# First products of a two-layer trunk's MLPs computed token-wise, their outputs turned by VectorE and a DRAM scratch

## The chip, the core and the metric

The kernel runs on one core of one Trainium2 chip. A core has TensorE for matrix products (into PSUM), VectorE (DVE) and ScalarE (ACT) for work on elements, GpSimd (POOL), SyncE (SP), which issues DMAs here, and 16 DMA engines between the device's memory (DRAM) and the core's SBUF. Each engine serves its own queue in order and waits on semaphores. The metric is the device time of one execution in microseconds, smaller is better. The program was run three times; one further execution was recorded by the hardware profiler, and all rows below come from it.

## What is computed

256 tokens of width 2048 go through two layers. In each layer a mixer (recurrent in the first, latent attention in the second, with a memory attention beside it) is followed by an MLP with squared ReLU, each between two RMS norms with a residual. Cut to the part that the change touches:

```python
D_MODEL = 2048; SEQ = 256; DEPTH = 2; D_FF = 4 * D_MODEL

def rms_norm(x, g):
    xf = x.astype(jnp.float32)
    xf = xf * lax.rsqrt(jnp.mean(xf * xf, axis=-1, keepdims=True) + EPS)
    return xf.astype(x.dtype) * g

def reference(x, mem, positions, ...):
    h = x
    for layer in range(DEPTH):
        ...
        h = h + rms_norm(y, g_mix_post[layer])
        f = rms_norm(h, g_mlp_pre[layer]) @ w_ff1[layer]
        f = jnp.square(jax.nn.relu(f)) @ w_ff2[layer]
        h = h + rms_norm(f, g_mlp_post[layer])
    return h
```

All of it is float32: w_ff1 is 2048 x 8192 and w_ff2 8192 x 2048 in each layer.

## The kernel before

**Products in three parts.** A float32 value is held as a high part, rounded to TensorE's fast float32 type, and a low part, the rest. A product is the sum of high x high, high x low and low x high. Weights come from DRAM as raw tiles of 128 x 1024 (`wraw`, five buffers, line 167, on SP's queue), ScalarE casts each to `whi` (line 129) and VectorE subtracts to get `wlo` (line 136), four buffers each. One such tile is a *group*: for 512 output columns it holds two k-tiles of 128 rows. `feed_high` and `feed_low` convert and load as far ahead as the buffers allow: a conversion waits until TensorE has used the group four back, a load until VectorE has converted the raw tile five back.

**Two forms of a product.** `gemm` walks over the groups of one weight block. *Feature-wise* (`by_features`) the weights are the stationary operand and the tokens run past: for each k-tile and each 128 features one matmul of 512 columns, token high and low parts side by side (line 235), and one of 256 (line 236). The output has features on partitions, in one PSUM bank for each 128 features; the two halves of a bank are added afterwards (`join`, lines 289 and 291: ScalarE copies a half to `corr`, VectorE adds). *Token-wise* (`by_tokens`) 128 tokens are stationary and the weights run past: for each k-tile and each of the two token halves three matmuls of 512 columns (lines 247 to 249). The output has tokens on partitions.

**The MLP.** `mlp` cuts the 8192 hidden features into NB = 8 blocks of 1024. `up(b)` makes block b from X, the normed tokens (features on partitions), in two products of 512 features, sixteen k-tiles, eight groups each; `down(b, F)` multiplies it with its rows of w_ff2 in four products of 512 columns, four groups each, token-wise, and adds up in `y`. The second product needs hidden features on partitions, which is how the feature-wise first product leaves them. The order is up(0), up(1), down(0), up(2), down(1), ... up(7), down(6), down(7). After the last matmul of each 128 features `ev` joins the two halves into `fs`; `square` then makes max(s, 0) x s on VectorE (line 726), casts the high part on ScalarE (line 727) and subtracts for the low part (line 729), into a tile F of 512 features.

**The order of the work.** It is written out by hand. Work beside the products stands as generators in a queue `bg`: at each group `run(1)` starts one more of them and takes each that has yielded 1 a step further, ahead of that group's conversion on VectorE and its load on SP, and behind its cast on ScalarE; `run(2)` does so behind the group's matmuls for those that yielded 2. So a step's place in an engine's queue is set by the group in which it falls.

**The second MLP's start.** The last product of the mixer before it is made with its second token half behind the first (`Mixed`), so that residual, transposes of `h` on TensorE (line 604) and split into high and low parts of the first token half run beside the second half's matmuls. The last four transposes and parts of X stand right ahead of up(0).

## Time and profile before

| | |
|---|---|
| median of three runs | 2126.18 us (2125.41 to 2127.99) |
| profiled execution | 2128.45 us |
| its span, from the first to the last instruction | 2126.7 us |
| TensorE, VectorE, ScalarE busy | 2092.9, 1326.0, 1074.0 us |
| DMA | 403.36 MB, 190 GB/s on average |

Busy time of TensorE is counted from a matmul's start to its modelled end; matmuls overlap, so a busy share near one says that there are few holes, not how fast the matmuls follow each other. How far apart they start is read from the timeline, and how long a stage lasts from the start of its first matmul to the start of the next stage's first.

### The profile page before, as it was taken

Reading aid. Unit: us, or ns where it says so; the run is one execution under the profiler, and the core shown is the slowest. Engines: PE = TensorE matmul, PEld = TensorE weight load, DVE = VectorE, ACT = ScalarE, POOL = GpSimd, SP = SyncE. Lnnn points to the kernel's source line nnn. Section 1 sums busy time; section 2 is a strip of 40 time slices with the busy share of each in tenths; the row PEclk is TensorE's granted clock in tenths of the full one; section 3 lists DMA queues with packets and bytes.
Section 4 is the critical chain, followed back from the end, with each engine's and each line's share of the span. In section 5 each row is a group of like instructions: output and inputs, shape, how many; then the busy total and the mean of one; then the engine's idle time right before and its main releaser. Section 6 shows DMA issues by size and latency. Waiting matters only on the chain. (4 is left out here: it accounts for less than half of the span.)

```text
span 2126.7 us, 29075 instructions
## 1 busy us (share of the span) xinstructions
PE 2092.9 (98%) x11055; PEld 1796.3 (84%) x11055; DVE 1326.0 (62%) x1960; ACT 1074.0 (50%) x1677; POOL 81.9 (4%) x124
## 2 busy tenths in 40 slices
PE   8999999999999999999999999999999999999998
PEld 6888888888888888888889898888888888888886
DVE  5688856764656656566576766576555656556565
ACT  6577645654444444444467655464543444434443
POOL 2311100000000000000010000000000000000001
PEclk9999999999999999999999999999999999999999
DMA  9565765666666666668656544656666666666664
GB/s 347 160 177 170 246 196 182 189 187 193 190 189 190 187 190 190 189 194 266 192 153 190 150 141 149 201 170 187 191 186 196 189 189 190 187 192 190 191 189 129
DMA packets 208604, 403.36 MB, mean 190 GB/s; under 512 B 12614, under 2 KB 31184, under 8 KB 206416
## 3 DMA queue, kind: packets, MB, share of 16 engines
q1 hardware_dynamic: 204720, 381.99, 60.5%
q0 software_dynamic: 3168, 18.47, 2.4%
q8 instruction: 86, 1.41, 0.3%
q10 hardware_dynamic: 576, 1.05, 0.1%
q14 instruction: 54, 0.44, 0.1%
HBM read 395.16 MB, written 6.29 MB: 189 GB/s over the span
## 5 line engine op out<-in xcount | busy, mean ns | idle before, releaser
L136 DVE TENSOR_TENSOR wlo<-wraw,whi 128x1024 fp32r<-128x1024 f32 x662 | 811.6, 1227 | 666.0 <-ACT whi L129 665.5
L129 ACT CAST whi<-wraw 128x1024 fp32r<-128x1024 f32 x662 | 692.4, 1046 | 832.1 <-PE psa L249 364.5
L235 PE MATMUL psb<-X,whi 128*128 128x512 f32 x2808 | 1002.7, 401 | 4.7 <-DVE ga L291 3.8
L236 PE MATMUL psb<-X,wlo 128*128 128x256 f32 x2808 | 788.8, 281 | 0.0
L235 PEld LDWEIGHTS psb<-X,whi 128*128 128x128 f32 x2808 | 528.8, 188 | 135.0 <-DVE ga L291 4.7
L247 PE MATMUL psa<-whi,X 128*128 128x512 f32 (+3 forms) x1636 | 605.8, 370 | 1.5 <-ACT whi L131 1.3
L248 PE MATMUL psa<-wlo,X 128*128 128x512 f32 (+3 forms) x1636 | 602.8, 368 | 0.6 <-DVE wlo L136 0.6
L249 PE MATMUL psa<-whi,X 128*128 128x512 f32 (+3 forms) x1636 | 602.6, 368 | 0.0
L236 PEld LDWEIGHTS psb<-X,wlo 128*128 128x128 f32 x2808 | 531.6, 189 | 1.1
L247 PEld LDWEIGHTS psa<-whi,X 128*128 128x128 f32 x1636 | 309.0, 189 | 52.8 <-ACT whi L131 1.7
L248 PEld LDWEIGHTS psa<-wlo,X 128*128 128x128 f32 x1636 | 308.9, 189 | 50.2 <-DVE wlo L136 1.0
L249 PEld LDWEIGHTS psa<-whi,X 128*128 128x128 f32 x1636 | 308.9, 189 | 50.1
L289 ACT COPY corr<-psb 128x256 f32<-128x256 f32 x192 | 68.6, 373 | 33.4 <-PE psb L236 33.2
L751 DVE SCALAR_TENSOR_TENSOR y<-psa,r,y 128x512 f32<-128x512 f32 (+1 forms) x114 | 79.2, 734 | 1.6 <-PE psa L249 1.5
L138 DVE SCALAR_TENSOR_TENSOR wlo<-wraw,pB,whi 128x384 fp32r<-128x384 f32 (+2 forms) x80 | 44.0, 599 | 23.0 <-ACT whi L131 22.8
L729 DVE TENSOR_TENSOR X<-fs,X 128x256 fp32r<-128x256 f32 x128 | 53.6, 419 | 0.0
L726 DVE SCALAR_TENSOR_TENSOR fs<-fs 128x256 f32<-128x256 f32 x128 | 53.5, 418 | 0.0
L138 DVE SCALAR_TENSOR_TENSOR wlo<-wraw,pM,whi 128x512 fp32r<-128x512 f32 x64 | 45.5, 755 | 12.8 <-ACT whi L131 12.5
L131 ACT ACTIVATE whi<-wraw,pB 128x384 fp32r<-128x384 f32 (+2 forms) x80 | 43.0, 597 | 17.2 <-PE psa L249 15.5
L727 ACT CAST X<-fs 128x256 fp32r<-128x256 f32 x128 | 51.3, 401 | 0.0
L291 DVE TENSOR_TENSOR fs<-psb,corr 128x256 f32<-128x256 f32 x128 | 48.2, 418 | 1.5
L131 ACT ACTIVATE whi<-wraw,pM 128x512 fp32r<-128x512 f32 x64 | 42.4, 718 | 10.0 <-PE psa L249 5.0
(279 smaller groups left out, 752.8 us busy)
## 6 DMA issues: line engine op xcount, KB each, us to landing
wraw<-in_w_ff_dram SPq DMA_DIRECT2D x512, 512.0 KB, 3.7
wraw<-in_w_o_dram SPq DMA_DIRECT2D x64, 512.0 KB, 3.8
wraw<-in_a_w_in_dram SPq DMA_DIRECT2D x56, 512.0 KB, 3.8
wraw<-in_w_mem_k_dram SPq DMA_DIRECT2D x16, 512.0 KB, 5.4
X<-mem_x POOLq DMA_DIRECT2D x8, 1024.0 KB, 10.4
wraw<-in_w_mem_v_dram SPq DMA_DIRECT2D x15, 512.0 KB, 4.7
wraw<-in_b_w_qb_dram SPq DMA_DIRECT2D x18, 384.0 KB, 3.1
wraw<-in_b_w_in_dram SPq DMA_DIRECT2D x16, 384.0 KB, 3.3
```

Of the source, the lines that this page charges most:

```text
L129: nc.scalar.copy(out=dst_hi, in_=src)
L131: nc.scalar.activation(dst_hi, src, AF.Copy, scale=g)
L136: nc.vector.tensor_tensor(out=dst_lo, in0=src, in1=dst_hi.bitcast(F32), op=ALU.subtract)
L138: nc.vector.scalar_tensor_tensor(out=dst_lo, in0=src, scalar=g, in1=dst_hi.bitcast(F32), op0=ALU.mult, op1=ALU.subtract)
L235: nc.tensor.matmul(psb[j], hi[:, k, b : b + P], Xk, start=first, stop=False)
L236: nc.tensor.matmul(psb[j][:, 256:512], lo[:, k, b : b + P], Xk[:, 0:256], start=False, stop=last)
L247: nc.tensor.matmul(psa[t], xh, a(hi[:, k, :]), start=first, stop=False, **kw)
L248: nc.tensor.matmul(psa[t], xh, a(lo[:, k, :]), start=False, stop=False, **kw)
L249: nc.tensor.matmul(psa[t], xl, a(hi[:, k, :]), start=False, stop=last, **kw)
L289: nc.scalar.copy(out=c, in_=ps[:, 256:512])
L729: nc.vector.tensor_tensor(out=F[:, j, 256:512], in0=s, in1=F[:, j, 0:256].bitcast(F32), op=ALU.subtract)
L751: nc.vector.scalar_tensor_tensor(out=dst, in0=ps, scalar=r2[:, t : t + 1], in1=dst, op0=ALU.mult, op1=ALU.add)
```

## The change

The first products of both MLPs become token-wise: `ev` applies the ReLU on ScalarE to a whole 128 x 512 bank, writing the columns in another order, into a tile `fs` for both token halves. As the hidden features are now on the free axis, `swap` turns them: `square` squares on VectorE; one group later VectorE transposes `fs` in squares of 32 x 32 into `sw_st`, and a DMA writes that to a DRAM scratch `on_way`; two groups later four DMAs read it back, 32 partitions each, in runs of 512 bytes, into `sw_got`, which now has features on partitions; two groups later ScalarE casts the high part, and one group later VectorE subtracts for the low part, both over 128 x 1024. `fs` and `sw_got` share one buffer, `sw_st` has one, `on_way` two. `corr` has three buffers, was four.

```diff
@@ -285,7 +285,7 @@
 
     def join(dst, ps, rows=None):
 
-        c = sp.tile([P, T], F32, name="corr", tag="corr", bufs=4)
+        c = sp.tile([P, T], F32, name="corr", tag="corr", bufs=3)
         nc.scalar.copy(out=c, in_=ps[:, 256:512])
         if rows is None:
             nc.vector.tensor_tensor(out=dst, in0=ps[:, 0:256], in1=c, op=ALU.add)
@@ -340,6 +340,28 @@
         yield 1
         for hi, lo, ps, g in todo:
             low(lo, hi, ps, g)
+
+    def swap(X, s, pool):
+
+
+        st = pool.tile([P, NT, 512], F32, name="sw_st", tag="sw_st", bufs=1)
+        for t in range(NT):
+            nc.vector.transpose(st[:, t, :], s[:, t, :])
+        on_way = dp.tile([NT, P, 512], F32, name="on_way", tag="on_way", bufs=2)
+        nc.sync.dma_start(out=on_way.rearrange("t p n -> p t n"), in_=st)
+        yield 1
+        yield 1
+        got = pool.tile([P, NT * 4, P], F32, name="sw_got", tag="fs", bufs=1)
+        for j in range(4):
+            src = on_way.rearrange("t (i f) n -> f (t i) n", i=4)[:, :, j * P : (j + 1) * P]
+            nc.sync.dma_start(out=got[32 * j : 32 * (j + 1)], in_=src)
+        yield 1
+        yield 1
+        hi, lo = (X[:, :, c : c + T].rearrange("p k (i r) -> p k i r", i=8) for c in (0, T))
+        got = got.rearrange("p i (k r) -> p k i r", k=4)
+        high(hi, got)
+        yield 1
+        low(lo, hi, got)
 
     def features(X, src, r, gain):
 
@@ -718,21 +740,23 @@
             for c in range(2):
                 F.append(xtile())
 
-                def ev(j, ps, F=F[-1]):
-                    s = scr(T, "fs")
-                    join(s, ps)
-
-                    def square():
-                        nc.vector.scalar_tensor_tensor(out=s, in0=s, scalar=0.0, in1=s, op0=ALU.max, op1=ALU.mult)
-                        nc.scalar.copy(out=F[:, j, 0:256], in_=s)
-                        yield 1
-                        nc.vector.tensor_tensor(
-                            out=F[:, j, 256:512], in0=s, in1=F[:, j, 0:256].bitcast(F32), op=ALU.subtract
-                        )
-
-                    bg.append(square())
-
-                gemm(UP[l][b][c], X, bcols=(0, 128, 256, 384), evac_b=ev)
+                def ev(t, ps, F=F[-1], got=[]):
+                    if t == 0:
+                        got.append(yp.tile([P, NT, 512], F32, name="fs", tag="fs", bufs=1))
+                    s = got[-1]
+                    ps = ps.rearrange("p (k j f) -> p j k f", k=4, j=4)
+                    dst = s[:, t, :].rearrange("p (j k f) -> p j k f", j=4, k=4)
+                    nc.scalar.activation(dst, ps, AF.Relu)
+                    if t == 1:
+                        bg.append(square(F, s))
+
+                def square(F, s):
+                    for t in range(NT):
+                        nc.vector.tensor_tensor(out=s[:, t, :], in0=s[:, t, :], in1=s[:, t, :], op=ALU.mult)
+                    yield 1
+                    yield from swap(F, s, yp)
+
+                gemm(UP[l][b][c], X, a=lambda w: w, evac_a=ev)
             return F
 
         def down(b, F):
```

SP's queue behind the first up product of the first MLP. Before, it holds weight loads alone (DMAHWn is the completion count of one of eight lanes, DVE_49 VectorE's count):

```order
L167 DMA wraw_3991<-in_w_ff1_dram 128x2x512 [waits DMAHW0_49,DVE_49]
L167 DMA wraw_4016<-in_w_ff1_dram 128x2x512 [waits DMAHW1_49,DVE_49]
L167 DMA wraw_4041<-in_w_ff1_dram 128x2x512 [waits DMAHW2_49,DVE_49]
L167 DMA wraw_4066<-in_w_ff1_dram 128x2x512 [waits DMAHW3_49,DVE_49]
L167 DMA wraw_4089<-in_w_ff1_dram 128x2x512 [waits DMAHW4_49,DVE_49]
```

After, the scratch write and the gather stand among them:

```order
L167 DMA wraw_3940<-in_w_ff1_dram 128x2x512 [waits DMAHW0_49,DVE_49]
L351 DMA on_way_3961<-sw_st_3958 128x2x512 [waits DMASW2_49,DMASW1_49,DMASW3_49,DMASW0_49,DMASW4_49,DVE_49,DMASW7_49,PE_49,Pool_49]
L167 DMA wraw_3965<-in_w_ff1_dram 128x2x512 [waits DMAHW1_49,DVE_49]
L167 DMA wraw_3983<-in_w_ff1_dram 128x2x512 [waits DMAHW2_49,DVE_49]
L357 DMA sw_got_3999<-on_way_3961 32x8x128 [waits DMAHW6_49]
L357 DMA sw_got_3999<-on_way_3961 32x8x128
L357 DMA sw_got_3999<-on_way_3961 32x8x128 [waits DMAHW3_49]
L357 DMA sw_got_3999<-on_way_3961 32x8x128 [waits DMAHW4_49]
L167 DMA wraw_4006<-in_w_ff1_dram 128x2x512 [waits DMAHW5_49,DVE_49]
L167 DMA wraw_4024<-in_w_ff1_dram 128x2x512 [waits DVE_49]
```

Each load behind row `on_way` leaves after VectorE's transposes, and the load behind the four `sw_got` rows after the write has landed (DMAHW6).

ScalarE's queue at the same place, before: four copies of a bank's half, then one cast of an F part behind each of the next weight casts:

```order
L289 COPY corr_3953<-psb_3691 128x256
L289 COPY corr_3961<-psb_3692 128x256
L289 COPY corr_3969<-psb_3693 128x256
L289 COPY corr_3977<-psb_3694 128x256
L129 CAST whi_3985<-wraw_3839 128x1024
L727 CAST X_3690<-fs_3952 128x256
L129 CAST whi_4009<-wraw_3873 128x1024
L727 CAST X_3690<-fs_3960 128x256
L129 CAST whi_4034<-wraw_3897 128x1024
```

After:

```order
L749 ACTIVATE fs_3924<-psa_3702 128x512 [waits PE_49]
L749 ACTIVATE fs_3924<-psa_3703 128x512 [waits PE_49]
L129 CAST whi_3934<-wraw_3825 128x1024 [waits DMAHW0_49,Activation_49]
L129 CAST whi_3956<-wraw_3855 128x1024 [waits DMAHW1_49,PE_49,Activation_49]
L129 CAST whi_3979<-wraw_3875 128x1024 [waits DMAHW2_49,DVE_49,PE_49]
L129 CAST whi_3997<-wraw_3896 128x1024 [waits DMAHW3_49,DVE_49,PE_49]
L129 CAST whi_4020<-wraw_3916 128x1024 [waits DMAHW4_49,DVE_49,PE_49]
L129 CAST whi_4038<-wraw_3940 128x1024 [waits DMAHW5_49,DVE_49,PE_49]
L129 CAST X_3690<-sw_got_3999 128x4x256 [waits DMAHW3_49,DMAHW2_49,DMAHW4_49,DMAHW1_49,DMASW6_49]
L129 CAST whi_4057<-wraw_3965 128x1024 [waits DMAHW7_49,DVE_49,PE_49]
L129 CAST whi_4076<-wraw_3983 128x1024 [waits DMAHW0_49,DVE_49,PE_49]
L749 ACTIVATE fs_4088<-psa_3942 128x512 [waits DVE_49,PE_49]
```

The two Relus stand ahead of the next weight cast, and the cast of the gathered tile, which waits for the four gather DMAs (lanes 1 to 4), stands six weight casts behind them, ahead of two more and of the next product's Relus (the first of them is the last row).

TensorE's queue at the start of the second MLP, before (the transposes of the second token half's first quarter, then the first pairs of up(0)):

```order
L604 MATMUL aux_12956<-ident_77,h_93 128x128 x2
L604 MATMUL aux_12959<-ident_77,h_93 128x128 x2
L235 MATMUL psb_12986<-X_12876,whi_12880 128x512
L236 MATMUL psb_12986<-X_12876,wlo_12884 128x256
L235 MATMUL psb_12986<-X_12876,whi_12880 128x512
L236 MATMUL psb_12986<-X_12876,wlo_12884 128x256
L235 MATMUL psb_12987<-X_12876,whi_12880 128x512
L236 MATMUL psb_12987<-X_12876,wlo_12884 128x256
```

After:

```order
L626 MATMUL aux_12236<-ident_77,h_93 128x128 [waits DVE_49,PE_49]
L626 MATMUL aux_12236<-ident_77,h_93 128x128
L626 MATMUL aux_12239<-ident_77,h_93 128x128 x2
L247 MATMUL psa_12282<-whi_12160,X_12156 128x512 [waits Activation_49]
L248 MATMUL psa_12282<-wlo_12164,X_12156 128x512
L249 MATMUL psa_12282<-whi_12160,X_12156 128x512
L247 MATMUL psa_12282<-whi_12160,X_12156 128x512 [waits Activation_49]
L248 MATMUL psa_12282<-wlo_12164,X_12156 128x512
L249 MATMUL psa_12282<-whi_12160,X_12156 128x512
L247 MATMUL psa_12283<-whi_12160,X_12156 128x512 [waits Activation_49]
L248 MATMUL psa_12283<-wlo_12164,X_12156 128x512
```

The transposes stay where they were; behind them now stand six matmuls on the first token half (the first PSUM bank) and then six on the second, where each matmul took both halves before.

## Rows read from the trace of the kernel before

**Rows 1.** The page: busy times, granted clock and DMA share in tenths by slice.
```profile
PE 2092.9 (98%) x11055; PEld 1796.3 (84%) x11055; DVE 1326.0 (62%) x1960; ACT 1074.0 (50%) x1677; POOL 81.9 (4%) x124
...
PEclk9999999999999999999999999999999999999999
...
DMA  9565765666666666668656544656666666666664
```

**Rows 2.** Timeline, TensorE, up product: start us, duration us, engine, line, names.
```profile
900.12 0.40 PE L235 MATMUL psb<-X,whi 128*128 128x512 f32 x1
...
905.78 0.40 PE L235 MATMUL psb<-X,whi 128*128 128x512 f32 x1
```

**Rows 3.** Timeline of a down product: TensorE, ScalarE's and VectorE's halves of a conversion.
```profile
912.82 0.39 PE L249 MATMUL psa<-whi,X 128*128 128x512 f32 x1
...
913.05 0.39 PE L247 MATMUL psa<-whi,X 128*128 128x512 f32 x1
...
913.29 1.05 ACT L129 CAST whi<-wraw 128x1024 fp32r<-128x1024 f32 x1 [1.36 <-issue]
...
914.38 1.22 DVE L136 TENSOR_TENSOR wlo<-wraw,whi 128x1024 fp32r<-128x1024 f32 x1 [0.82 <-ACT whi L129]
...
915.54 0.39 PE L249 MATMUL psa<-whi,X 128*128 128x512 f32 x1
```

**Rows 4.** Windows (length, five engines' busy time, clock, DMA share, GB/s): up, down, up.
```profile
507.16:552.37 45.21, 45.21 (x257) 39.23 (x256) 24.14 (x30) 20.89 (x28) 0.00 (x0) 1.00 0.64 189
...
552.37:595.95 43.58, 43.58 (x194) 36.05 (x193) 27.35 (x34) 18.37 (x21) 0.00 (x0) 1.00 0.67 192
...
951.13:996.34 45.21, 45.21 (x258) 39.24 (x257) 25.26 (x32) 20.32 (x27) 1.63 (x3) 1.00 0.75 236
```

**Rows 5.** Waits: who waited for whom, us in total, times, longest.
```profile
ACT whi L129 <- PE psa L249: 364.5, 223, 4.3
```

**Rows 6.** Timeline, TensorE, the memory values' product.
```profile
1106.29 0.39 PE L249 MATMUL psa<-whi,X 128*128 128x512 f32 x1
...
1109.69 0.39 PE L249 MATMUL psa<-whi,X 128*128 128x512 f32 x1
```

**Rows 7.** Timeline, TensorE, start of the second MLP.
```profile
1399.94 0.63 PE L604 MATMUL aux<-ident,h 128*128 128x128 f32 x4 [2.85 <-DVE h L563]
...
1401.46 0.67 PE L235 MATMUL psb<-X,whi 128*128 128x512 f32 x1 [0.88 <-DVE X L138]
```

**Rows 8.** Groups by form: xcount | busy us, mean ns | idle before, releaser.
```profile
L289 ACT COPY corr<-psb 128x256 f32<-128x256 f32 x192 | 68.6, 373 | 33.4 <-PE psb L236 33.2
...
L727 ACT CAST X<-fs 128x256 fp32r<-128x256 f32 x128 | 51.3, 401 | 0.0
...
L726 DVE SCALAR_TENSOR_TENSOR fs<-fs 128x256 f32<-128x256 f32 x128 | 53.5, 418 | 0.0
...
L749 ACT ACTIVATE y<-psa,r 128x512 f32<-128x512 f32 x16 | 11.1, 691 | 7.2 <-PE psa L249 7.2
...
L136 DVE TENSOR_TENSOR X<-aux,X 128x512 fp32r<-128x512 f32 x16 | 10.5, 687 | 3.4 <-ACT X L129 3.4
```

**Rows 9.** Waits of SP's queue.
```profile
SPq L167 <- DVE wlo L136: 1372.7, 561, 7.9
```

**Rows 10.** DMA issues: names, queue, count, KB each, median us to landing.
```profile
wraw<-in_w_ff_dram SPq DMA_DIRECT2D x512, 512.0 KB, 3.7
...
X<-mem_x POOLq DMA_DIRECT2D x8, 1024.0 KB, 10.4
...
mem_x<-X POOLq DMA_DIRECT2D x4, 1024.0 KB, 8.2
...
gw<-in_a_w_rgate_dram POOLq DMA_DIRECT2D x3, 256.0 KB, 3.5
...
gw<-in_a_w_igate_dram POOLq DMA_DIRECT2D x3, 256.0 KB, 5.0
```

**Rows 11.** Windows, columns as in rows 4: the memory tiles being loaded.
```profile
992.00:1004.00 12.00, 12.00 (x60) 10.09 (x59) 8.74 (x14) 6.41 (x11) 0.53 (x1) 1.00 1.04 389
```

## The prediction, made before the changed kernel was run

> **What bounds the kernel now.** I read the page's busy shares first: TensorE is busy for 98% of the span, VectorE for 62%, ScalarE for 50%, TensorE's clock is full in nearly every slice, and the DMA engines stand at about six tenths [rows 1]. So the time is a count of matmuls times the distance between their starts, plus a few stalls. Durations of single matmuls overlap each other and can't be summed (one of 0.39 us starts 0.23 us after the one before) [rows 3]; the distance between starts has to come from the timeline.
>
> Next, that distance, in the two forms that a product can have. In the first products ("up") a feature-wise pair, one of 512 columns (line 235) and one of 256 (line 236), goes out every 353 ns: from 900.12 to 905.78 us there are 16 pairs [rows 2]. In the second products ("down") a token-wise matmul of 512 columns (lines 247 to 249) goes out every 227 ns: from 912.82 to 915.54 us there are twelve [rows 3]. Both forms push the same columns for one k-tile of 512 features, 4 x 768 = 6 x 512 = 3072, but the first takes 4 x 353 = 1413 ns and the second 6 x 227 = 1362 ns. The stages confirm it: a whole up(b) lasts 45.21 us (256 matmuls), the down behind it 43.58 us (192), with a clock of 1.00 and TensorE busy throughout, and a later up(b) takes 45.21 us again [rows 4].
>
> Then, who waits. ScalarE's longest wait in total, 364.5 us, is that of a weight conversion for TensorE to let go of a buffer [rows 5]: the conversions run as far ahead as their four buffers allow. In a steady group of weights the conversion begins at 913.29, 0.24 us after the group's first matmul (913.05), and VectorE's half ends at 914.38 + 1.22 = 915.60 [rows 3]; TensorE needs it three groups later, 3 x 2.72 = 8.16 us after 913.05, so at 921.2. That is a reserve of 5.6 us for anything that delays ScalarE or VectorE for a moment.
>
> **The change, part by part.** *The up products become token-wise.* An up(b), two products, then has the instructions, shapes, operand roles and group length of a down(b): 192 matmuls of 512 columns for 256 of 512 and 256. I price it at the down's 43.58 us, so 1.63 us less per up(b), and 2 layers x 8 = 16 of them: **-26.0 us**. That this pace belongs to the form and not to the down is borne out by a third stage: the memory values, token-wise too, have 15 starts from 1106.29 to 1109.69 us, 227 ns each [rows 6].
>
> Here the Trainium skill speaks against the change. The page "TensorE: Matmul & The Clock Gate", section "Wait — 56ns, not 53.3ns?", puts back-to-back matmuls at N / 2.4 GHz plus about 2.5 ns (215.7 ns at 512 columns). By that rule the gain would be two instructions per k-tile, 2 x 2.5 ns x 512 k-tiles = 2.6 us, an estimate from that page. The rows disagree: 227 ns, and 353 ns for a pair that the rule puts near 325 [rows 2, 3].
>
> *The start of the second MLP.* Before, TensorE stands still behind its four transposes (1399.94) until 1401.46, because a feature-wise matmul wants both token halves of X, and the last of them is VectorE's [rows 7]. After, six matmuls on the first token half, finished long before, stand right behind the transposes (order, below the diff), so TensorE can start at about 1400.6: up to 0.9 us. The next groups wait for VectorE's work on the other quarters of X, which comes no earlier, so a part may be given back. Bounds 0 and 0.9; I take **-0.4 us**.
>
> *Evacuation.* Per up product ScalarE loses four corr copies (373 ns) and four casts (401 ns), 3.1 us; VectorE loses twelve passes over 128x256 at 418 ns (four each of lines 291, 726 and 729, of which one row stands), 5.0 us [rows 8]. ScalarE gains two Relus of 128x512 (nearest row 691 ns) and a cast of 128x1024 (1.05 us), 2.4 us; VectorE gains two squarings (nearest 687 ns), two square-wise transposes, which no row shows, and a subtraction of 128x1024 (1.22 us) [rows 3, 8]. The transposes: at least 0.42 us each (half the elements), at most 1.22 us (twice as many); I take the 0.69 us of the same size. VectorE's new work is then 4.0 us, bounds 3.4 to 5.1. Neither engine sets the pace: in the timeline both have gaps in each group [rows 3], so this counts **0**. If the reserve of 5.6 us were gone, every microsecond of these would count.
>
> *The detour through DRAM.* Per product one DMA of 512 KB out and four of 128 KB back in runs of 512 B, all on SP's queue, where SP stands waiting for VectorE most of the time (1372.7 us in all) [rows 9]. Behind them in SP's queue stand the weight loads, and behind those the conversions. In us from the last matmul of an up product, in groups of weights of 2.72 us: the Relus end at 0.9, the squarings at 1.6, one conversion's subtraction at 3.2, the transposes at 4.6, when the out DMA leaves. Landing: 3.7 us is the row for a weight load of 512 KB, 8.2 for 1 MB from SBUF to DRAM [rows 10]; I take 4.0, near the one of the same size, so 8.6. The gather stands in group 3 (8.16) and goes at 8.6. Nearest row: two loads of gate weights, 256 KB each in 512 B runs, issued one right behind the other (about 0.8 us) and landing 3.5 and 5.0 us after issue, so 512 KB in 5.8 us [rows 10]: it lands at 14.4. ScalarE comes to the cast of the gathered tile in group 5, after one conversion, at 5 x 2.72 + 0.3 + 1.05 = 14.95. It waits for nothing. A late gather first eats the reserve: behind it stand its cast (1.05), its subtraction and that of the next weights on VectorE (2 x 1.22) and some 0.3 us of handing over, 3.8 us, and those weights are wanted at 9 x 2.72 = 24.5; so TensorE begins to stall when the gather lands after about 20.7. SP held for some us costs nothing either, a raw tile being loaded five groups (13.6 us) before its conversion and landing in 3.7. The result is wanted only after the 16 groups of the next down. **0 us**, bounds 0 and, with both slowest rows (8.2 out, 10.4 back [rows 10]), 4.6 + 8.2 + 10.4 = 23.2, 2.5 us of stall x 32 = 80 us.
>
> *DMA bandwidth.* 1.05 MB more per product are 2.1 MB in 87 us, 24 GB/s beside 190. The up(b) from 951.13 us, beside which the memory tiles were loaded, had 236 GB/s and still took 45.21 us [rows 4]; from 992 to 1004 us the DMA engines stood at 1.04 of their time and TensorE was busy all through [rows 11]. **0 us**.
>
> *corr with three buffers for four.* The four joins of a product come two feature-wise pairs apart, 0.71 us, and VectorE's add takes 0.42 us; the 192 copies waited 33.2 of 33.4 us for TensorE [rows 8]. **0**, at most some tenths for about ten products.
>
> **Sum.** 26.0 + 0.4 = 26.4 us less. The profiled execution took 2128.45 us (its span 2126.7, the rest lies around it), which gives 2102.0 for the like. The median of the three runs is 2126.18, 2.3 us below the profiled one, so I forecast **2099.8 us** for the median. About 0.2%, 4.3 us, is what a measurement of this kernel can tell from no change.
>
> **The rivals.** *Late gather (slower).* ScalarE serves its queue in order; if the gather lands after 20.7 us, the weight conversions queue behind the cast and TensorE stalls once per product. It decides the sign at 0.83 us of stall (26.4 / 32), a landing at about 21.5, seven us later than I have it. With both slowest rows: 2099.8 + 80 = 2180 us. For it: two transfers in series, with the first's landing before the second's issue, among weight loads. Against: both slow rows are of 1 MB, twice this size, and the second with the DMA engines full [rows 11].
>
> *Partly late, or some other stall of a few tenths per product.* 0.2 to 0.6 us x 32 = 6 to 19 us, 2106 to 2119 us. For it: the price of a VectorE transpose and of the writes are not in the trace.
>
> *The pace belongs to the stage and not to the form* (the change doesn't do what it says). Then up stays at 45.21 us and only the 0.4 us are left: 2125.8 us. Against it: the memory values [rows 6]. By the rule of the Trainium skill's page "TensorE: Matmul & The Clock Gate" named above the time would be 2126.2 - 2.6 - 0.4 = 2123.2, an estimate that falls on this side too; rows 2 and 3 speak against it.
>
> **How the numbers follow.** Forecast 0.79; partly late 0.09; pace of the stage 0.04; late gather 0.08. The forecast's own range is 2097 to 2103 (start of the second MLP 0 to 0.9 us, the 2.6 us between the three runs). With half of the partly late case, low 2095 and high 2109 hold 0.8. Faster 0.88, same 0.04, slower 0.08.
>
> **What would show it.** In the profile after: up(b) stretches of 43.6 us with token-wise starts every 227 ns and no 256-column matmuls in them; ScalarE's cast from the gathered tile without a wait for a DMA in the list of waits; gather landings under 8 us; VectorE transposes near 0.7 us; DMA share near 0.72 in these stages. It would be wrong if TensorE showed a hole once per product, waiting for a converted weight behind ScalarE's cast, or if starts in the up stages stayed further apart than 227 ns.

## The result, and the profile after

| | before | after |
|---|---|---|
| median on the same chip | 2125.8 us (4 runs) | 2099.61 us (2097.89 to 2099.88, 4 runs) |
| profiled execution | 2128.45 us | 2099.88 us |
| its span | 2126.7 us | 2097.8 us |

The ratio is 0.9875, 95% interval 0.9858 to 0.9892: 26.2 us faster. The forecast was 2099.8 us. The sum was right. Of its steps two were too small (the pace of the up products and the start of the second MLP), and two were wrong (that ScalarE waits for nothing, and that the DMA engines are nowhere too full); the wrong ones cost 2 us at one place. The next sections take them apart.

The page of the changed kernel, in the form of [rows 1] (busy time, share and instructions of each engine; granted clock and DMA share in tenths by slice):

```profile
PE 2064.2 (98%) x10031; PEld 1744.6 (83%) x10031; DVE 1305.5 (62%) x1736; ACT 1058.5 (50%) x1517; POOL 81.9 (4%) x124
...
PEclk9999999999999999999999999999999999999999
...
DMA  9555755786776767778656444658776767777673
```

TensorE has 1024 matmuls fewer (16 up stages x 64) and is as full as before; VectorE and ScalarE did not become fuller; the DMA engines went from about six tenths to seven. The windows of one up, the down behind it, and the one down that was disturbed, in the form of [rows 4]:

```profile
501.57:545.09 43.52, 43.52 (x194) 36.06 (x193) 23.42 (x22) 20.18 (x21) 0.00 (x0) 1.00 0.72 219
545.09:588.61 43.52, 43.52 (x194) 36.06 (x193) 26.91 (x28) 18.21 (x18) 0.00 (x0) 1.00 0.73 218
...
980.28:1025.78 45.50, 44.33 (x194) 35.91 (x192) 30.27 (x31) 21.32 (x22) 0.53 (x1) 1.00 0.85 284
```

An up stage now lasts what a down stage lasts, 43.52 us for 45.21 before. The down itself went from 43.58 to 43.52: the 0.06 us had lain in its first ten matmuls, behind the last feature-wise pair. The start of the second MLP, TensorE's timeline, for [rows 7]:

```profile
1386.06 0.63 PE L626 MATMUL aux<-ident,h 128*128 128x128 f32 x4 [2.85 <-DVE h L585]
1386.45 0.48 PE L247 MATMUL psa<-whi,X 128*128 128x512 f32 x1
...
1387.36 0.63 PE L247 MATMUL psa<-whi,X 128*128 128x512 f32 x1
...
1389.92 0.63 PE L247 MATMUL psa<-whi,X 128*128 128x512 f32 x1
```

The first product begins 0.39 us behind the start of the last transposes, where it was 1.52 us.

**Where the 28.9 us between the two spans went**, from the starts of TensorE's matmuls: 8 x 1.69 = 13.5 in the first MLP's up stages; 13.1 in the second's (1.27 in up(0), which runs partly at half clock in both kernels, seven times 1.69 in the rest); 0.8 in fourteen down stages; 1.1 at the second MLP's start; 2.0 given back in the down that begins at 980.28. That is 26.6 from the unrounded values. The rest stands before the first MLP, where the two kernels are alike, and differs from run to run: over the profiles of the changed kernel and its variants the first MLP begins between 369.6 and 373.2 us.

Now the detour. Groups of the page (count | busy us, mean ns | idle before, and its releaser), and DMA issues (KB each, median us to landing):

```profile
L136 DVE TENSOR_TENSOR X<-sw_got,X 128x1024 fp32r<-128x1024 f32 x32 | 39.2, 1226 | 68.9 <-ACT X L129 68.9
...
L129 ACT CAST X<-sw_got 128x1024 fp32r<-128x1024 f32 x32 | 33.6, 1050 | 74.5 <-DMA sw_got<-on_way 74.5
...
L749 ACT ACTIVATE fs<-psa 128x512 f32<-128x512 f32 x64 | 38.2, 598 | 31.5 <-PE psa L249 30.9
...
L755 DVE TENSOR_TENSOR fs<-fs 128x512 f32<-128x512 f32 x64 | 43.7, 688 | 11.3 <-ACT fs L749 11.3
...
on_way<-sw_st SPq DMA_DIRECT2D x32, 512.0 KB, 4.5
sw_got<-on_way SPq DMA_DIRECT2D x128, 128.0 KB, 6.3
```

The transposes, by tile (minimum, median and longest ns):

```profile
L349 DVE STREAM_TRANSPOSE sw_st<-fs x64: 667/688/708, 395.7 to 2004.2; 128x512 f32<-128x512 f32 x64
```

And the waits of ScalarE and of SP's queue (us in total, times, longest), beside [rows 5] and [rows 9]. In the kernel before, ScalarE's weight casts waited for TensorE under two lines, 364.5 us for line 249 and 274.2 us for the feature-wise line 235; now nearly all of it stands under one:

```profile
ACT whi L129 <- PE psa L249: 693.7, 445, 4.3
...
ACT X L129 <- DMA sw_got<-on_way: 74.5, 32, 8.0
```

```profile
SPq L167 <- DVE wlo L136: 1343.4, 588, 9.7
...
SPq L351 <- DVE sw_st L349: 25.0, 32, 0.8
...
SPq L357 <- DMA on_way<-sw_st: 18.9, 25, 2.5
```

ScalarE waits for the gather at every one of the 32 products, 2.3 us on average. It was said to wait for nothing. TensorE pays for it at one place only. This is a timeline of all engines there; the four loads of the memory tiles (line 804, GpSimd's queue, 1 MB each) are issued from 964.66 to 980.96, and the DMA share (before the GB/s, behind the clock) stands above 1:

```profile
964.00:981.00 17.00, 17.00 (x77) 14.08 (x76) 4.90 (x4) 4.22 (x4) 1.67 (x4) 1.00 1.04 306
```

```profile
980.96 0.53 POOL L804 DMA_DIRECT2D X<-mem_x  x1 [4.91 <-issue]
...
981.35 1.05 ACT L129 CAST X<-sw_got 128x1024 fp32r<-128x1024 f32 x1 [7.96 <-DMA sw_got<-on_way]
...
982.30 1.99 ACT L129 CAST whi<-wraw 128x1024 fp32r<-128x1024 f32 x2
...
982.78 0.39 PE L249 MATMUL psa<-whi,X 128*128 128x512 f32 x1
...
983.39 0.50 PE L247 MATMUL psa<-whi,X 128*128 128x512 f32 x1 [0.22 <-ACT whi L129]
...
984.84 0.50 PE L248 MATMUL psa<-wlo,X 128*128 128x512 f32 x1 [0.95 <-DVE wlo L136]
```

The cast waited 7.96 us, the weight cast stood behind it, TensorE ran out of converted weights, and the down stage took 45.50 us.

### The profile page after: what moved, and what is told of

It is laid out like the page before. It is cut to its first block, busy times and chain, and to the rows that moved or that the text cites. A ratio compares the mean times of both kernels' runs of the same rounds, so it can differ in the third digit from the quotient of the medians.

```text
span 2097.8 us, 26951 instructions
## 1 busy us (share of the span) xinstructions
PE 2064.2 (98%) x10031; PEld 1744.6 (83%) x10031; DVE 1305.5 (62%) x1736; ACT 1058.5 (50%) x1517; POOL 81.9 (4%) x124
## 5 line engine op out<-in xcount | busy, mean ns | idle before, releaser
L247 PE MATMUL psa<-whi,X 128*128 128x512 f32 (+3 forms) x2660 | 1005.4, 378 | 1.7 <-ACT whi L131 1.3
L248 PE MATMUL psa<-wlo,X 128*128 128x512 f32 (+3 forms) x2660 | 1002.3, 377 | 1.5 <-DVE wlo L136 1.5
L249 PE MATMUL psa<-whi,X 128*128 128x512 f32 (+3 forms) x2660 | 1002.2, 377 | 0.0
L247 PEld LDWEIGHTS psa<-whi,X 128*128 128x128 f32 x2660 | 501.3, 188 | 92.7 <-ACT whi L131 1.7
L248 PEld LDWEIGHTS psa<-wlo,X 128*128 128x128 f32 x2660 | 501.4, 188 | 91.5 <-DVE wlo L136 2.5
L249 PEld LDWEIGHTS psa<-whi,X 128*128 128x128 f32 x2660 | 501.2, 188 | 89.5
L235 PE MATMUL psb<-X,whi 128*128 128x512 f32 x760 | 277.5, 407 | 3.8 <-DVE ga L291 3.8
L236 PE MATMUL psb<-X,wlo 128*128 128x256 f32 x760 | 213.7, 281 | 0.0
L235 PEld LDWEIGHTS psb<-X,whi 128*128 128x128 f32 x760 | 143.6, 189 | 37.7 <-DVE ga L291 4.7
L236 PEld LDWEIGHTS psb<-X,wlo 128*128 128x128 f32 x760 | 144.7, 190 | 0.7
L136 DVE TENSOR_TENSOR X<-sw_got,X 128x1024 fp32r<-128x1024 f32 x32 | 39.2, 1226 | 68.9 <-ACT X L129 68.9
L129 ACT CAST X<-sw_got 128x1024 fp32r<-128x1024 f32 x32 | 33.6, 1050 | 74.5 <-DMA sw_got<-on_way 74.5
L755 DVE TENSOR_TENSOR fs<-fs 128x512 f32<-128x512 f32 x64 | 43.7, 688 | 11.3 <-ACT fs L749 11.3
```

The costliest lines, as they stand in the source:

```text
L129: nc.scalar.copy(out=dst_hi, in_=src)
L136: nc.vector.tensor_tensor(out=dst_lo, in0=src, in1=dst_hi.bitcast(F32), op=ALU.subtract)
L235: nc.tensor.matmul(psb[j], hi[:, k, b : b + P], Xk, start=first, stop=False)
L236: nc.tensor.matmul(psb[j][:, 256:512], lo[:, k, b : b + P], Xk[:, 0:256], start=False, stop=last)
L247: nc.tensor.matmul(psa[t], xh, a(hi[:, k, :]), start=first, stop=False, **kw)
L248: nc.tensor.matmul(psa[t], xh, a(lo[:, k, :]), start=False, stop=False, **kw)
```

## The experiments

All times are medians; the kernel before, run beside each of the three sets, had 2126.83, 2126.31 and 2126.25 us. Intervals are 95% intervals of the ratio to it.

### Is the detour free?

The changed kernel without the detour (line numbers as in its own text):

```diff
-        st = pool.tile([P, NT, 512], F32, name="sw_st", tag="sw_st", bufs=1)
...
-            nc.sync.dma_start(out=got[32 * j : 32 * (j + 1)], in_=src)
-        yield 1
-        yield 1
+        for _ in range(4):
+            yield 1
...
-        got = got.rearrange("p i (k r) -> p k i r", k=4)
+        got = s.rearrange("p t (i k r) -> p (t i) k r", i=4, k=4).rearrange("p i k r -> p k i r")
```

> The changed kernel with the detour left out: no square-wise transposes, no scratch write, no gather; ScalarE and VectorE cast and subtract from the squared tile itself, in the same groups as before (the hidden features then stand in the wrong places). Theory (the detour is hidden but for one stall of 1.95 us in the first MLP's down(6)): about 2097.7 us against 2099.6 of the changed kernel, every up and down stage 43.52 us, ScalarE's 74.5 us of waits for the gather gone. Rival (the detour costs some tenths per product, 0.1 to 0.3 x 32): 2090 to 2096 us.

Measured: 2098.71 us (ratio 0.9869, 0.9852 to 0.9885), beside 2099.96 for the changed kernel in the same set. The rival is out: the detour's 64 transposes, 32 writes and 128 gathers together cost 1.25 us of 2100 by the medians, whose runs overlap, and 2.0 us by the stages of the traces, all of it in one down stage. The memory tiles are still loaded, and the stretch that was disturbed before is not now:

```profile
960.00:1010.00 50.00, 50.00 (x223) 41.40 (x222) 30.11 (x29) 22.73 (x25) 2.17 (x4) 1.00 0.81 280
980.50:1026.00 45.50, 45.50 (x202) 37.72 (x201) 27.38 (x27) 19.48 (x20) 0.53 (x1) 1.00 0.73 248
```

So the 2 us belong to gather and memory tiles together: the loads of the memory tiles without a gather beside them delay nothing.

### How much reserve is there before the gather's delay reaches TensorE?

Three kernels move ScalarE's cast of the gathered tile against the gather, by groups of 2.72 us: one group later (one more `yield 1` ahead of `high(hi, got)`), one earlier, two earlier (one or both taken out).

> The changed kernel with one more group between the gather and ScalarE's cast of the gathered tile (the cast in group 6, the subtraction in group 7). Theory (the only price of the gather is ScalarE's wait in order, and it stalls TensorE only where it exceeds a reserve of about 6 us): waits for the gather shrink by 2.72 us each, from 74.5 us to below 12 in total, the longest from 8.0 to about 5.3, the stall of 1.95 us goes: about 2097.7 us. Rival (that stall comes from weight loads which are late while the memory tiles fill the DMA engines): the stall stays, 2099.6 us.

> The changed kernel with one group less between gather and cast (the cast in group 4). Theory (a reserve of about 6 us): each of ScalarE's 32 waits grows by 2.72 us, from 2.3 to 5.0 us on average; only the few longest get past the reserve, 5 us more in all: about 2105 us (2102 to 2109). Rival (ScalarE's waits cost TensorE nothing, or the reserve is far larger): 2099.6 us. Rival (there is no reserve, each wait counts): 32 x 2.72 = 87 us more, 2187 us.

> The changed kernel with ScalarE's cast of the gathered tile in the group of the gather itself (group 3). Theory (a reserve of about 6 us): the 32 waits grow by 5.44 us to 7.8 on average, 1.8 us past the reserve: 43 to 69 us of stalls, 2140 to 2167 us, with TensorE waiting for a converted weight once per product. Rival (ScalarE's waits cost TensorE nothing): 2100 us.

Measured, with the line from each one's list of waits below:

| cast | time, us | ratio | ScalarE waits for the gather | TensorE |
|---|---|---|---|---|
| one later | 2098.06 | 0.9868 (0.9854 to 0.9883) | 14.3 us, 5 times | the one stall near 985 |
| as it is | 2099.96 | 0.9876 (0.9861 to 0.9891) | 74.5 us, 32 times | the one stall near 984 |
| one earlier | 2106.02 | 0.9908 (0.9893 to 0.9922) | 157.0 us, 32 times | the one stall, 3.1 us idle |
| two earlier (second set) | 2139.13 | 1.0059 (1.0039 to 1.0079) | 233.4 us, 32 times | late at 30 of 32 products |

```profile
ACT X L129 <- DMA sw_got<-on_way: 14.3, 5, 8.4
```

```profile
ACT X L129 <- DMA sw_got<-on_way: 157.0, 32, 9.9
```

```profile
ACT X L129 <- DMA sw_got<-on_way: 233.4, 32, 15.6
```

(from the top: one later, one earlier, two earlier). Each group earlier adds 2.4 to 2.6 us to the mean wait, where 2.72 us was expected. The single waits give the reserve, if TensorE's lateness is taken from the distances between its starts (what they have beyond 0.227 us, added up behind each cast); its idle time hides part of it, as a matmul's modelled end moves along. In the kernel with the cast one group earlier, for one, a wait of 6.51 us goes with starts 0.38 and 0.34 us apart and no idle time at all:

```profile
1741.70 1.05 ACT L129 CAST X<-sw_got 128x1024 fp32r<-128x1024 f32 x1 [6.51 <-DMA sw_got<-on_way]
```

```profile
1744.81 0.39 PE L247 MATMUL psa<-whi,X 128*128 128x512 f32 x1
1745.19 0.50 PE L248 MATMUL psa<-wlo,X 128*128 128x512 f32 x1
1745.53 0.40 PE L249 MATMUL psa<-whi,X 128*128 128x512 f32 x1
```

| ScalarE's wait, us | TensorE's starts late by, us | difference | kernel |
|---|---|---|---|
| up to 6.17 | 0 | | changed kernel, one later, one earlier |
| 6.41, 7.96 | 0.18, 1.72 | 6.23, 6.25 | changed kernel |
| 8.23 | 1.98 | 6.25 | changed kernel, second profile |
| 6.63, 6.93 | 0.38, 0.69 | 6.25, 6.24 | changed kernel, third profile |
| 8.40 | 2.15 | 6.25 | one later |
| 6.26, 6.51 | 0.02, 0.27 | 6.24, 6.25 | one earlier |
| 6.41 to 7.89 (27 products) | 0.18 to 1.67 | 6.22 to 6.25 | two earlier |

So the reserve is 6.25 us at each of these products, where [rows 3] had given 5.6 and the sum 20.7 - 14.95 = 5.8, and what goes beyond it TensorE loses one for one. Four waits cost more. Two of 9.86 and 15.58 us, at the memory tiles with the cast one and two groups earlier, cost 5.2 and 11.9 us, as the clock fell behind them; two of 7.50 and 6.86 us with the cast two groups earlier cost 1 us more than that, and why is open. With the cast two groups earlier the mean wait is 233.4 / 32 = 7.3 us and TensorE stalls as the rival "late gather" said it would, behind the weight cast and its subtraction:

```profile
481.31 0.50 PE L247 MATMUL psa<-whi,X 128*128 128x512 f32 x1 [0.91 <-ACT whi L129]
482.57 0.50 PE L248 MATMUL psa<-wlo,X 128*128 128x512 f32 x1 [0.76 <-DVE wlo L136]
```

That kernel is slower than the kernel before: the rival's mechanism is real, and it lay two groups of weights away. Its 2139.13 us are just under the expected 2140, and of TensorE's 38.8 us of lateness 11.9 are those at the memory tiles. Of the 6.1 us that the cast one group earlier costs, 3.3 are lost at the memory tiles (its first MLP lasts 696.5 us up to the same matmul, for 693.2), where it stalls longer and the clock falls to 0.67 in the window from 986 to 988 us and to 0.50 in the next, 0.4 in the down stages of the second MLP, and 1.9 stand before the first MLP, where the two kernels are alike: so the traces give the earlier cast some 3.7 us, and the rest of the 6.1 is what varies.

The cast one group later did not remove the stall at the memory tiles, though its expectation said that it would (longest wait 5.3 us, waits below 12 us in all): there the gather itself took up to 14.8 us to land, and the cast still waited 8.40 us for it. That the stall stayed is what the rival of late weight loads forecast, but its reason is not the one: TensorE was late by what the wait for the gather had beyond 6.25 us, and without the gather there was no stall.

### What is it at the memory tiles?

First the whole detour in the kernel before, beside its feature-wise products (a generator like `square` and `swap` on a tile of ones, once per product; its result goes nowhere):

```diff
+                    nc.vector.transpose(st[:, t, :], s[:, t, :])
...
+                nc.sync.dma_start(out=on_way.rearrange("t p n -> p t n"), in_=st)
...
+                    nc.sync.dma_start(out=got[32 * j : 32 * (j + 1)], in_=src)
...
+                nc.scalar.copy(out=st, in_=got)
...
-                    bg.append(square())
+                    bg.append((detour(), square()) if j == 0 else square())
```

> The kernel before, feature-wise, with the whole detour beside each up product: a tile of ones transposed by VectorE, written to the scratch, gathered, copied by ScalarE and subtracted by VectorE in the same groups as in the change, its result not used (corr with three buffers as well). Theory (the gain is the products' form alone, the detour is hidden): 2125.8 us plus 0 to 2, up stages 45.21 us. Rival (the detour costs TensorE something wherever it stands): 3 to 10 us more, 2129 to 2136.

Measured: 2137.54 us, ratio 1.005 (1.0033 to 1.0067), 11.2 us more than the 2126.31 us of the kernel before beside it (10.7 in a text below is the distance to the 2126.83 of the first set). That is above what either side expected. Its up stages last 45.21 us as before; 10.0 us of the loss are in one down stage, 53.59 us for 43.58. ScalarE, TensorE, and the window behind it:

```profile
999.19 1.04 ACT L737 COPY sw_st<-sw_got 128x1024 f32<-128x1024 f32 x1 [10.81 <-DMA sw_got<-on_way]
```

```profile
1004.15 0.79 PE L247 MATMUL psa<-whi,X 128*128 128x512 f32 x1 [6.90 <-DVE fs L291]
```

```profile
994.00:1002.00 8.00, 3.25 (x17) 2.39 (x15) 1.74 (x2) 2.81 (x3) 0.53 (x1) 0.87 1.12 377
1002.00:1010.00 8.00, 5.85 (x14) 4.59 (x15) 7.89 (x15) 4.12 (x9) 0.00 (x0) 0.50 0.72 229
```

The DMA engines stand at 1.12, the gather lands late, ScalarE, waiting for it, cannot evacuate the up product's banks, TensorE stands 6.90 us and then works at half clock.

Then the loads of the memory tiles were moved away from the gathers, in this kernel and in the one with the cast one group later: from GpSimd's queue to SP's, in the last down stage, where no product is turned:

```diff
+    def mem_paced(X):
+        for _ in range(1):
+            yield 1
+        for q in range(4):
+            X.append(xtile())
+            nc.sync.dma_start(out=X[-1].bitcast(F32), in_=mem_x[q].bitcast(F32))
+            yield 1
+            yield 1
+            yield 1
...
-    y, ss = mlp(0, XF, yp, first=[rope_tables(yp)], then=lambda: mem_again(XM2))
+    y, ss = mlp(0, XF, yp, first=[rope_tables(yp)], then=lambda: bg.append(mem_paced(XM2)))
```

> The kernel before with the whole detour (transposes, write, gather, cast, subtraction) beside its feature-wise products, its result not used, and with the four loads of the memory tiles in SP's queue in the last down product, three groups apart, instead of beside a gather. With those loads beside the gather it took 2137.5 us, 10.7 more than before, and the trace put all of it into one hole and the half clock behind it. Theory (that place is the whole price of the detour here): 2126 to 2128 us. Rival (the detour's work costs at every product, some tenths each): 2130 us or more, the hole gone and the rest still there.

Measured: 2126.45 us, ratio 0.9999 (0.999 to 1.0009), where the same detour had cost 11.2 us. The rival is out: apart from that one place the detour costs nothing beside feature-wise products, although ScalarE waits 69.1 us in all for its gathers (29 times, at most 3.6). Place and queue of the loads were changed together, so which of the two frees the gather is not shown apart.

```profile
994.00:1010.00 16.00, 16.00 (x73) 13.23 (x73) 14.48 (x25) 8.39 (x12) 0.00 (x0) 1.00 0.84 234
```

> The changed kernel with the cast of the gathered tile one group later, and with the four 1-MB loads of the memory tiles taken from GpSimd's queue, where they all run beside the last gather but one of the first MLP, to SP's queue in the last down product, three groups apart, where no gather runs. Theory (the detour costs only where those loads take the DMA engines from a gather, 1.4 to 1.9 us there): no idle time of TensorE around 960 to 1010 us, ScalarE's waits for the gathered tile under 15 us with none above 3, 2098.1 - 1.5 = 2096.6 us (2096 to 2097.5). Rival (the loads delay whatever they run beside): the loads behind which weight loads now stand on SP's queue make holes of 1 us or more in the last down product, 2098 us or more.

> The changed kernel again, beside the kernel with the loads of the memory tiles moved: 2098.5 to 2100.5 us; the difference between the two is read from this call.

> The changed kernel itself, on the same chip as its variants. Both theories: 2099.6 us, 1.25% below the kernel before.

Measured: 2099.22 us (0.987, 0.9854 to 0.9885) for the paced kernel, 2098.97 (0.9871, 0.9853 to 0.9888) for the changed kernel beside it, 2099.96 (0.9876) for it in the first set. In the trace the theory is right: the stall is gone, the down stage lasts 43.52 us (45.50, 45.51 and 44.64 in the three profiles of the changed kernel), and ScalarE's waits for the gather are

```profile
ACT X L129 <- DMA sw_got<-on_way: 1.7, 4, 0.8
```

for 14.3 with the cast one group later alone and 74.5 in the changed kernel. In the time it does not show: 1.1 to 2 us is less than what the rest varies by. In this very profile, for one, the half clock at the start of the second MLP lasted 6.8 us, in that of the changed kernel beside it 3.4, and the stage was 0.7 us longer. The expectation of 2096.6 us was therefore missed, and no version here is shown to beat the changed kernel.

### Why does a token-wise product take less time?

The same columns are pushed in either form. To part the number of instructions from the form, token-wise matmuls of the changed kernel's up stages were cut into two of 256 columns, and the feature-wise ones of the kernel before into three of 256:

```diff
+                    for x, w, f, l in ((xh, hi, first, False), (xh, lo, False, False), (xl, hi, False, last)):
+                        for c in (0, 256):
+                            nc.tensor.matmul(
+                                psa[t][:, c : c + 256], x, w[:, k, c : c + 256],
```

> The changed kernel with each 512-column matmul of the up products cut in two of 256 columns, the same columns and results with twelve matmuls per k-tile for six. Theory (start distance = columns / 2.4 GHz plus a fixed 13 to 14 ns per matmul; 256-column matmuls of the mixer's last product start 0.120 us apart in the trace): 12 x 120 = 1440 ns for 6 x 227 = 1360 per k-tile, 80 ns x 512 = 41 us more, 2140 us, up stages 46.1 us. Rival (the Trainium skill, page TensorE: Matmul & The Clock Gate, section Wait - 56ns, not 53.3ns?, about 2.5 ns per matmul): 6 x 2.5 x 512 = 8 us more, 2107 us.

```diff
+                        nc.tensor.matmul(psb[j][:, 0:256], w, Xk[:, 0:256], start=first, stop=last, **kw)
+                        nc.tensor.matmul(psb[j][:, 256:512], w, Xk[:, 256:512], start=False, stop=False, **kw)
+                        nc.tensor.matmul(psb[j][:, 256:512], lo[:, k, b : b + P], Xk[:, 0:256], start=False, stop=last, **kw)
```

> The kernel before, feature-wise, with the 512-column matmul of the up products cut in two of 256, so that a k-tile takes twelve matmuls of 256 columns, as many as the token-wise variant cut the same way. Theory (only the number and length of matmuls count): 3 x 120 = 360 ns for the 353 of a pair, 7 ns x 2048 = 14 us more than the kernel before, 2140 us, up stages 46.1 us, the same as the cut token-wise variant. Rival (the feature-wise form costs some 3 ns more per matmul, whatever its length): 3 x 123 = 369 ns, 33 us more, 2159 us, up stages 47.2 us.

Measured: 2137.5 and 2140.59 us. TensorE's timelines, token-wise and then feature-wise; between the first and the last line there are ten matmuls in each:

```profile
699.73 0.64 PE L250 MATMUL psa<-whi,X 128*128 128x256 f32 x4
700.21 0.40 PE L250 MATMUL psa<-wlo,X 128*128 128x256 f32 x2
700.45 0.64 PE L250 MATMUL psa<-whi,X 128*128 128x256 f32 x4
700.93 0.40 PE L250 MATMUL psa<-wlo,X 128*128 128x256 f32 x2
```

```profile
700.08 0.28 PE L238 MATMUL psb<-X,whi 128*128 128x256 f32 x1
...
701.28 0.28 PE L239 MATMUL psb<-X,wlo 128*128 128x256 f32 x1
```

Both go out every 120.0 ns, and the up stages last 46.07 us in both kernels; the 3 us between the two times lie outside them, most of it ahead of the first MLP (it begins at 370.65 and at 373.51 us). At full clock (2.4 GHz) 256 columns are 106.7 ns and 512 are 213.3, so the rest is 13.3 ns at 256 and, with 226.7, 13.3 ns at 512: one price per matmul, whatever its width and form. The form itself counts nothing; what a k-tile pays for is the number of its matmuls. The rule that the prediction weighed, 2.5 ns (the Trainium skill, "TensorE: Matmul & The Clock Gate", section "Wait — 56ns, not 53.3ns?"), would have put the cut token-wise kernel at 2107 us, an estimate; the run, 2137.5, decides against it for this stream.

A feature-wise pair of 512 and 256 takes 353.3 ns, though, and 226.7 + 120.0 are 346.7. In the feature-wise kernel whose matmuls all have 256 columns nothing is left over, so the 6.7 ns belong to the mixture. To see whether they come from the change of length, the kernel before was given both 512-column matmuls of two k-tiles first and then both of 256:

```diff
+                    for k in range(len(ks)):
+                        nc.tensor.matmul(psb[j], hi[:, k, b : b + P], Xs[k], start=(i, k) == (0, 0), stop=False)
+                    for k in range(len(ks)):
+                        last = (i, k) == (last_group, len(ks) - 1)
+                        nc.tensor.matmul(psb[j][:, 256:512], lo[:, k, b : b + P], Xs[k][:, 0:256], start=False, stop=last)
```

> The kernel before, with its feature-wise products kept, but of each pair of k-tiles the two 512-column matmuls first and then the two 256-column ones. A pair took 353.3 ns where two matmuls of 512 columns take 2 x 226.7 and two of 256 columns 2 x 120.0, so 346.7 for one of each: 6.7 ns per pair are left over, 2 x 8 x 128 x 1 x 2 = 2048 pairs in both layers' up products, 13.7 us in all. Theory: they belong to the change of length from one matmul to the next; half as many changes, 6.8 us less: 2119 to 2120 us. Rival: they belong to a pair for another reason (the 256-column matmul's own moving operand), then no change: 2125.8 us.

Measured: 2116.53 us (0.9952, 0.9937 to 0.9967), 9.7 us less than before; eighteen groups of two pairs lie between these two lines of TensorE's timeline:

```profile
869.76 0.62 PE L235 MATMUL psb<-X,whi 128*128 128x512 f32 x2
...
882.30 0.62 PE L235 MATMUL psb<-X,whi 128*128 128x512 f32 x2
```

That is 348.3 ns a pair, 5.0 less; 5.0 x 2048 = 10.2 us (16 up stages of 128 pairs), which agrees with the time. So order matters and the rival (no change) is out, but half as many changes of length took away three quarters of the 6.7 ns, not half, and 2116.53 us is below the expected 2119. Nor does the trace put what is left at the changes: from 850 to 890 us of the grouped kernel a matmul of 512 columns is followed, in the mean, after 232.7 ns by another of 512 and after 233.4 by one of 256 (226.7 in the token-wise stream), and one of 256 after 114.5 ns by another of 256 and after 115.9 by one of 512. The grouping also changed the order of the weights (two high parts, then two low ones). So that the change of length is the cause is not shown; it stays open.

With this the change's gain can be parted. A k-tile of 512 features took 1413 ns and takes 1360. Two matmuls fewer are 2 x 13.3 = 27 ns; four mixed pairs fewer are 4 x 6.7 = 27 ns. About half of the gain, then, goes with the mixture of lengths and half with the number of matmuls. Order alone, in the old form and without the detour, gave 9.7 of the 27 us.

## Why the prediction was right, step by step

- **The pace of the up products**, -26.0 us: the mechanism (TensorE is full, so the starts' distance is the time) was right and the size nearly. What the prediction called the pace of the form is not the form's: with 256 columns both forms keep 120.0 ns, and the gain is that of fewer matmuls of one length. A stage fell by 1.69 us, not 1.63, since the pace was taken from a down stage that still had a change of form beside it (43.58); the sixteen, one of them partly at half clock, gave 26.6 us. The choice to read the distance between starts instead of summing busy times carried this: TensorE's busy time fell by 28.7 us, but its shares stood at 98% in both kernels and told nothing. The rival "the pace belongs to the stage" is out: 43.52 us in every undisturbed stage.
- **The second MLP's start**, -0.4 us with bounds 0 and 0.9: 1.13 us, above its upper bound. The bound took for granted that the first matmul starts 0.7 us behind the first of the four transposes; it started 0.39 us behind it. Nothing of it was given back in the stage behind it, which also fell by 1.27 us.
- **Evacuation**, 0: right. The transposes took 688 ns where 0.69 us was taken; the Relu took 598 ns for 691; VectorE's busy time fell by 20.5 us.
- **The detour**, 0: right in the sum, with a wrong step. "It waits for nothing" was false at all 32 products. In the first product the write left 4.35 us behind the last matmul (said: 4.6) and landed in 4.3 us, 4.5 in the median (said: 4.0), so the gather was issued at 8.7 (said: 8.6): good. The term that was too small is the gather's own, 5.8 us for the lot: each of its four DMAs took 6.3 us in the median, and from the first issue to the cast it is 7.7 us in the first product (401.45 to 409.16 us). The cast began at 16.4 us there, at 17.0 in the median of the 32 products, instead of 14.95. By the prediction's own signs this one, a cast without a wait for a DMA, failed. What made the sum right is the other half of the step, the reserve: TensorE was said to stall from a landing at 20.7 us, 5.8 us of waiting, and does so from 6.25 us of it.
- **DMA bandwidth**, 0: wrong at one place, by 2.0 us. The rows that it rested on [rows 4, 11] were of a stretch in which nothing waited for a transfer within some microseconds. The changed kernel put such a transfer there, a gather, beside the same four loads.
- **Late gather** (0.08) did not happen but at that place; its mechanism and its price were shown by the cast two groups earlier. That the memory tiles would be the place where it starts was in the prediction's rows, and not drawn from them.
- **corr with three buffers**, 0: right as far as the up stages show, for they use it no more; by itself it was tried only as part of the detour beside feature-wise products, where the up stages kept 45.21 us.

The sum came out at 26.4, the traces give 26.6 up to what varies: 0.6 more (pace), 0.7 more (start), 0.8 more (the down stages) and 2.0 less (memory tiles) nearly cancel, which is luck in the last microsecond and not in the first twenty-five.

## What to carry to other kernels

Where TensorE is full, count matmuls and read the distance between their starts for each shape and mixture: at full clock each one here pays a fixed price beside its columns, and mixed lengths pay more, so the same columns in fewer, equal matmuls are faster, and the order of the matmuls is worth trying before a new form. A detour through DRAM can be free if its result is wanted late; what has to be worked out is the reserve of the queue that waits for it, and the one stretch where another bulk transfer takes the DMA engines. A wait on a busy engine is not yet a cost: with 74.5 us of it on ScalarE TensorE's starts were late by 1.9 us in all, with 157.0 by 5.5 and with 233.4 by 38.8, since each product has the same reserve of 6.25 us, and only what goes beyond it counts.

## What the runs showed of the hardware

**The fixed price is there only at full clock.** In both kernels the second MLP starts with some microseconds at a granted clock of 0.50 (1.2 GHz), behind TensorE's 2.85 us of idleness. In the kernel before, three pairs lie between these lines:

```profile
1402.14 0.63 PE L235 MATMUL psb<-X,whi 128*128 128x512 f32 x1
...
1404.06 0.63 PE L235 MATMUL psb<-X,whi 128*128 128x512 f32 x1
```

That is 640 ns a pair, which is 768 columns at 1.2 GHz and nothing else; in the changed kernel's lines from 1387.36 to 1389.92 us, shown above, six matmuls take 427 ns each, 512 columns at 1.2 GHz. So four pairs and six matmuls cost the same 2.56 us there, and what the change saves per k-tile it saves at the full clock alone. What limits the stream at 2.4 GHz by 13.3 ns a matmul no run here tells.

**A late transfer is paid for twice.** The stall of 6.90 us in the detour beside feature-wise products was followed by a window of 8 us at a clock of 0.50, so the place cost 10.0 us. With the cast one group earlier 3.1 us of idle time at the same place were followed by 0.50 as well; idle times of about 1 us in the changed kernel, as at 984.84, left the clock at 1.00. The windows with the cast one group earlier:

```profile
986.00:988.00 2.00, 2.00 (x6) 1.62 (x7) 2.00 (x2) 2.00 (x4) 0.00 (x0) 0.67 1.11 420
988.00:990.00 2.00, 2.00 (x6) 1.52 (x6) 2.00 (x4) 0.28 (x1) 0.00 (x0) 0.50 1.04 372
```

**Four small gathers take longer than one large write.** 128 KB in runs of 512 B took 6.3 us (4.1 to 11.7) to land, 512 KB written from SBUF 4.5 us (3.8 to 5.7), in the same stretches and on the same queue; with the DMA engines full the gather took up to 14.8 us. Size, direction and length of the runs differ between the two, and no run tells which counts.
